# Moving the overflow block of a mixture of experts from the end of the expert loop to its middle

## The chip, the cores and the metric

The kernel runs on one core of a Trainium2 chip. The metric is the device time of one execution in microseconds; of several runs the median is taken. A second number is the span of the one execution that was profiled, from its first to its last recorded instruction.

## What is computed

The reference is one encoder block over 1024 tokens of width 1024: two attention branches, a gated merge, a layer norm, and then a mixture of 16 experts with a second layer norm. The change touches only the mixture. Each token picks one group of four experts and two experts in it, so there are 2048 token-expert pairs, and the outputs are added with the token's weights:

```python
y = jnp.zeros_like(u)
for e in range(N_EXPERTS):
    h = jax.nn.silu(u @ w_gate[e]) * (u @ w_up[e])
    y = y + comb[..., e:e + 1] * (h @ w_down[e])
```

The kernel computes only the pairs that were chosen. With these inputs the reference's own routing gives the experts 0 to 15 these numbers of tokens: 38, 69, 18, 17, 46, 151, 122, 119, 188, 61, 143, 180, 218, 177, 195, 306.

## The kernel before, in words

Tokens of one expert are gathered in blocks of 128 rows. Every expert has a first block; a second one is computed only if it has more than 128 tokens (here experts 5, 8 and 10 to 15; expert 15 needs a third). Blocks past an expert's second go on a list that is worked out on the chip (`overflow_list`, L1500). The first entry of that list gets a step of its own after the sixteen experts, with a weight load whose expert number is read from a register (`w_dyn`, L1627); further entries would be handled by a loop after it (L1738), which here has no pass.

All matrix products are made in three passes: each operand is split into a rounded high part and the remainder (`halves`, L200; the split of a 128x1024 weight piece is a copy on ScalarE, `ewh`, and a subtraction on VectorE, `ewl`), and `mm3` (L141) multiplies low by high, high by low and high by high.

For a block the work is: gather the tokens' rows from memory (`gather`, L1538, an indirect DMA of GpSimd into `xg`); transpose them on TensorE and split them (`transpose_x`, L1544, tiles `pxt`, `xh`, `xl`); gate and up (`gate_up`, L1565: 24 matmuls into `pgu`, then silu on ScalarE and a product on VectorE into `sg`); transpose the hidden activations (`hidden`, L1582, tiles `pht`, `hh`, `hl`); down (`down`, L1591: 12 matmuls into two banks `pdn`); scale (two VectorE operations into `ot`, L1614); and add the rows to the sums in memory (L1615, an indirect DMA of GpSimd into `acc_d`). Where a block is left out, one or two stand-in matmuls (L1576, L1606) fill its banks.

Each scatter adds to the same tensor `acc_d`, so each waits until the one before it has landed. There are two `ot` tiles, so an `ot` is written only once the scatter before last has landed.

An expert's weights are 3 MB in six pieces of 512 KB (`load_expert`, L1409): pieces 0 to 3 for gate and up, 4 and 5 for down. SyncE's queue issues them in order. Two pools hold the raw pieces and their splits, 16 slots (`L`) and 14 (`X`); successive steps use them by turns, so even steps use `X` and odd ones `L`.

The order of the work inside the loop is written out by hand, and the scheduler keeps it on all engines (`manual_schedule`, L1685). The loop runs over steps, and in each over the letters of one string (L37):

```python
ORDER = 'A4B0bC1cDEPe2FG35g'
```

In step e: `A` transposes the hidden activations of e-1; `B` and `C` are gate and up of e's two blocks, `b` and `c` their silu and product; `D` and `F` transpose the two blocks of e+1; `E` and `G` are the downs of e-1's two blocks, `e` and `g` their scaling and scatter; `P` issues the gathers of e+3; the digits 0 to 3 split pieces of e+1's weights, 4 and 5 the last two pieces of e's. Before the change step 16 is the overflow block, and pass 17 only finishes it. After the loop the sums are read back (L1758), normalised and written out.

Of the kernel before, what the change touches and what calls it, by code (L numbers as in the profile page):

```python
# [25 lines left out]
T = 1024  # L26
# [4 lines left out]
NE = 16  # L31
# [55 lines left out]
def block_kernel(ctx: ExitStack, tc, a, out):  # L87
    nc = tc.nc
    V, S, G, PE = nc.vector, nc.scalar, nc.gpsimd, nc.tensor
    dma = nc.sync.dma_start  # L90
    ET = mybir.EngineType
# [9 lines left out]
    def s2(name, tag, shape=(128, 512), dt=FT):  # L101
        return sb.tile(list(shape), dt, name=name, tag=tag, bufs=HALVES[tag])
# [727 lines left out]
    A = {}  # L830
# [574 lines left out]
    ew, first_gather = {}, []  # L1405
# [71 lines left out]
    idxg = cp.tile([128, 129], U32, name="idxg")  # L1477
    idxs = cp.tile([128, 129], U32, name="idxs")
# [7 lines left out]
    wtab = cp.tile([128, 129], FT, name="wtab")  # L1486
# [10 lines left out]
    lsti = cp.tile([128, 40], I32, name="lsti")  # L1497
    cnti = cp.tile([128, 16], I32, name="cnti")
# [44 lines left out]

    def transpose_x(xg, xh=None, xl=None):  # L1544
        if xh is None:
            xh, xl = s4("xh", "wh", dt=FR), s4("xl", "wl", dt=FR)
        for hf in range(2):
            p = bank("pxt", "tp")
            for k in range(4):
                PE.transpose(p[:, k * 128:k * 128 + 128], xg[:, (hf * 4 + k) * 128:(hf * 4 + k) * 128 + 128], ident)  # L1550
            t = slice(hf * 512, hf * 512 + 512)
            copy(xh[:, t], p)
            sub(xl[:, t], p, xh[:, t])
        return xh, xl
# [10 lines left out]
    def gate_up(w, x, sg, cond_=None):  # L1565

        xh, xl = x
        p = bank("pgu", "lg")

        def some():  # L1570
            for k in range(KC):
                ws = slice((k % 2) * 512, (k % 2) * 512 + 512)
                wh, wl = w[k // 2]
                mm3(p, xh[:, k * 128:k * 128 + 128], xl[:, k * 128:k * 128 + 128], wh[:, ws], wl[:, ws], k == 0, k == KC - 1)

        only(cond_, some, lambda: PE.matmul(p, w[0][0][:, 512:640], w[0][0][:, 0:512], start=True, stop=True))  # L1576
        yield
        S.activation(sg, p[:, 0:256], AF.Silu)
        V.tensor_tensor(sg, sg, p[:, 256:512], op=OP.mult)
        yield  # L1580

    def hidden(sg, n):  # L1582
        p = bank("pht", "av", (128, 256 * n))
        for k in range(2 * n):
            PE.transpose(p[:, k * 128:k * 128 + 128], sg[:, k * 128:k * 128 + 128], ident)
        hh, hl_ = s2("hh", "pt", (128, 256 * n), FR), s2("hl", "pt", (128, 256 * n), FR)
        copy(hh, p)
        sub(hl_, p, hh)
        return [(hh[:, 256 * b:256 * b + 256], hl_[:, 256 * b:256 * b + 256]) for b in range(n)]

    def down(w, h, wcol, isc, cond_=None, cond_p=None):  # L1591
        hh, hl_ = h
        ot = s4("ot", "b")
        p = [bank("pdn", "mm") for _ in range(2)]

        def some():
            for f in range(2):
                fs = slice(f * 512, f * 512 + 512)
                for k in range(2):
                    hs = slice(k * 128, k * 128 + 128)  # L1600
                    wh, wl = w[4 + k]
                    mm3(p[f], hh[:, hs], hl_[:, hs], wh[:, fs], wl[:, fs], k == 0, k == 1)

        def none():
            for f in range(2):
                PE.matmul(p[f], hh[:, 0:128], w[4][0][:, 0:512], start=True, stop=True)  # L1606

        only(cond_, some, none)
        yield

        def finish():
            for f in range(2):
                fs = slice(f * 512, f * 512 + 512)
                V.scalar_tensor_tensor(ot[:, fs], p[f], wcol, g2r[f], op0=OP.mult, op1=OP.mult)  # L1614
            G.indirect_dma_start(out=acc_d, out_offset=bass.IndirectOffsetOnAxis(ap=isc, axis=0), in_=ot, in_offset=None,  # L1615
                                 compute_op=OP.add)

        where(cond_p and cond_p(), finish)
        yield
# [14 lines left out]
    def prefetch(e):  # L1634
        for b in range(2 if e < NE else 0):
            xg[e, b] = gather(idxg[:, e * 8 + b:e * 8 + b + 1], second(e) if b else None)
        if e == NE:
            xg[e, 0] = gather(ic0[:, 0:1])

    def transposed(e, b):  # L1640
        if (e, b) in xg:
            x = xg.pop((e, b))
            h, l = s4("xh", "wh", dt=FR), s4("xl", "wl", dt=FR)
            where(several(e) if b else None, lambda: transpose_x(x, h, l))
            xt[e, b] = h, l

    def several(e, engines=(ET.PE, ET.Activation, ET.DVE)):

        return nc.values_load(cnti[0:1, e:e + 1], engines=list(engines), min_val=0, max_val=T) > 128

    def load(e, q):
        if e <= NE:
            if q == 0:
                if e == NE:
                    e_r = nc.values_load(lsti[0:1, 16:17], engines=[ET.SP], min_val=0, max_val=NE - 1)
                gens[e] = load_expert((lambda q: a["w_exp"][e, :, q * 1024:q * 1024 + 1024]) if e < NE else lambda q: w_dyn(e_r, q),
                                      "LX"[(e + 1) % 2])
            ew[e] = next(gens[e])

    gens = {}  # L1660
    copy(cnti, cnt16, V)
# [23 lines left out]
    man = tc.manual_schedule(engines={ET.PE, ET.DVE, ET.Activation, ET.Pool, ET.SP})  # L1685
    man.__enter__()


    def gu(e, b):
        if e > NE or (e == NE and b):  # L1690
            return iter(())
        if b == 0:
            sgs[e] = s2("sg", "sg")
        if b or e == NE:
            counts[e] = nc.values_load(cnti[0:1, e:e + 1] if e < NE else lsti[0:1, 32:33], engines=[ET.PE], min_val=0, max_val=T)
        return gate_up(ew[e], xt.pop((e, b)), sgs[e][:, b * 256:b * 256 + 256],
                       counts[e] > 128 * b if b or e == NE else None)

    def dn(e, b):
        if e < 0 or (e == NE and b):  # L1700
            return iter(())
        if e == NE:
            return down(ew[e], hs_[e][b], wo0, ic0[:, 1:2], counts[e] > 0,
                        lambda: nc.values_load(lsti[0:1, 32:33], engines=[ET.DVE, ET.Pool], min_val=0, max_val=T) > 0)
        col = e * 8 + b
        return down(ew[e], hs_[e][b], wtab[:, col:col + 1], idxs[:, col:col + 1], counts[e] > 128 if b else None,
                    (lambda: several(e, (ET.DVE, ET.Pool))) if b else None)

    for e in range(NE + 2):
        for n, c in enumerate(ORDER):  # L1710
            if c == "P":
                prefetch(e + 3)
            if c == "A" and 0 < e:
                hs_[e - 1] = hidden(sgs.pop(e - 1), 2 if e <= NE else 1)
            if c in "BC":
                g = gu(e, "BC".index(c))
                next(g, None)
            if c in "bc":
                next(g, None)
            if c in "DF":  # L1720
                transposed(e + 1, "DF".index(c))
            if c in "EG":
                d = dn(e - 1, "EG".index(c))
                next(d, None)
            if c in "eg":
                next(d, None)
            if c in "012345":
                q = int(c)
                ee = e if q >= 4 else e + 1
                if ee > 1:  # L1730
                    load(ee, q)

    held[0] = None
    man.__exit__(None, None, None)
# [108 lines left out]
```

## Time and profile before

| quantity | value |
|---|---|
| runs of the kernel before | 1376.50, 1386.26, 1388.22 us, median 1386.26 us |
| the profiled execution | 1377.23 us, its span 1375.4 us |
| mean granted TensorE clock in it | 0.957 |
| gate and up of step 0 begin | 1048.4 us into the span |
| the last scatter lands | 1342.9 us |
| scatters | 24 of experts' blocks, 1 of the overflow block |

The profile has, beside a page for the whole execution, views that can be cut to a stretch of time: the busy time of each engine in a list of windows; the instructions of one engine in order of time, with the idle time ahead of an instruction and what ended it in brackets; and the chain of work that ended last, followed back from the last instruction. In a row of the timeline the first number is the start in microseconds from the beginning of the span, the second the duration. A matmul's duration overlaps with the next one's, so costs on TensorE are taken from start to start.

### The profile page before, as it was taken

The numbers are of one execution on the slowest core, as the hardware profiler recorded it, in microseconds if no ns is written. First come the engines' busy times: TensorE is split into PE (matmuls) and PEld (weight loads), VectorE is DVE, ScalarE is ACT, GpSimd is POOL, SyncE is SP. The second block draws the span as 40 slices with busy tenths as digits, with TensorE's granted clock in tenths as the row PEclk, the third lists the DMA queues.
The fourth block names the chain that finished last, engine by engine and source line by source line (L and its number), as shares of the span: only waits on it lengthen the run. The fifth ranks groups of instructions, "written<-read, shape, count | busy, mean of one in ns | idle before, by whom it ended". The sixth has DMA issues, their size and how long they took to land. (4 is left out here: it accounts for less than half of the span.)

```text
span 1375.4 us, 18536 instructions
## 1 busy us (share of the span) xinstructions
PE 1246.5 (91%) x6216; PEld 978.6 (71%) x6231; DVE 960.0 (70%) x2096; ACT 673.9 (49%) x1198; POOL 124.3 (9%) x154
## 2 busy tenths in 40 slices
PE   7999999999999999998889898999986888999950
PEld 6876678877777777667667777787874766788840
DVE  6537699783447668655676768887798677877736
ACT  4536662224785545445746556434224455654415
POOL 1000000000000001001001100000002222333120
PEclk9999999999999999999989998999997999999985
DMA  9212452123124317564445522674436788989856
GB/s 368 91 32 70 149 183 75 47 72 117 61 74 145 131 55 242 188 184 127 147 136 153 163 69 67 231 240 158 178 107 230 249 288 244 320 289 311 245 86 251
DMA packets 108487, 225.92 MB, mean 164 GB/s; under 512 B 33104, under 2 KB 39648, under 8 KB 108384
## 3 DMA queue, kind: packets, MB, share of 16 engines
q1 hardware_dynamic: 67952, 164.22, 33.9%
q0 software_dynamic: 35824, 52.03, 14.0%
q10 hardware_dynamic: 4608, 8.39, 1.9%
q8 instruction: 53, 0.87, 0.2%
q14 instruction: 50, 0.41, 0.1%
HBM read 169.94 MB, written 54.58 MB: 163 GB/s over the span
## 5 line engine op out<-in xcount | busy, mean ns | idle before, releaser
L142 PE MATMUL pj<-uh,wl 128*128 128x512 f32 x544 | 220.7, 406 | 1.8 <-ACT bkr L132 0.8
L145 PE MATMUL pj<-ul,wh 128*128 128x512 f32 x544 | 216.2, 398 | 0.0
L146 PE MATMUL pj<-uh,wh 128*128 128x512 f32 x544 | 215.8, 397 | 0.0
L128 DVE TENSOR_TENSOR ewl<-raw,ewh 128x1024 fp32r<-128x1024 f32 x102 | 122.7, 1219 | 35.8 <-ACT ewh L132 30.2
L132 ACT ACTIVATE ewh<-raw 128x1024 fp32r<-128x1024 f32 x102 | 105.5, 1056 | 60.8 <-DMA raw<-w_exp 60.4
L142 PEld LDWEIGHTS pj<-uh,wl 128*128 128x128 f32 x544 | 102.6, 189 | 35.1 <-issue 10.2
L146 PEld LDWEIGHTS pj<-uh,wh 128*128 128x128 f32 x544 | 102.4, 188 | 26.1 <-issue 5.6
L145 PEld LDWEIGHTS pj<-ul,wh 128*128 128x128 f32 x544 | 102.7, 189 | 23.6 <-issue 5.1
L132 ACT ACTIVATE pth<-ptr 128x512 fp32r<-128x512 f32 (+1 forms) x120 | 65.7, 551 | 71.2 <-PE ptr L793 40.0
L128 DVE TENSOR_TENSOR ptl<-ptr,pth 128x512 fp32r<-128x512 f32 (+1 forms) x120 | 75.4, 634 | 23.6 <-ACT pth L132 22.9
L142 PE MATMUL pgu<-ewh,xl 128*128 128x512 f32 x200 | 81.4, 407 | 1.0 <-DVE xl L128 0.8
L793 PE MATMUL ptr<-ident,P 128*128 128x128 f32 x432 | 73.0, 286 | 8.4 <-DVE ptl L128 7.1
L146 PE MATMUL pgu<-ewh,xh 128*128 128x512 f32 x200 | 79.4, 397 | 0.0
L145 PE MATMUL pgu<-ewl,xh 128*128 128x512 f32 x200 | 79.4, 397 | 0.0
L765 ACT ACTIVATE P<-P,mx 128x128 f32<-128x128 f32 (+7 forms) x64 | 49.4, 772 | 39.9 <-DVE mx L762 36.7
L1615 POOL DMA_INDIRECT acc_d<-ot,idxs x24 | 47.5, 1980 | 198.4 <-DVE ot L1614 135.8
L793 PEld LDWEIGHTS ptr<-ident,P 128*128 128x128 f32 x432 | 52.3, 146 | 16.6 <-DVE ptl L128 8.0
L128 DVE TENSOR_TENSOR wl<-raw,wh 128x512 fp32r<-128x512 f32 x68 | 44.9, 686 | 22.8 <-ACT wh L132 22.6
L780 ACT ACTIVATE P<-P,mx 128x128 f32<-128x128 f32 (+3 forms) x64 | 49.4, 772 | 21.8 <-DVE mx L778 20.7
L758 PE MATMUL plg<-ak,aq 64*128 64x512 f32 (+4 forms) x288 | 58.2, 375 | 1.3 <-DVE mx L762 1.3
L444 DVE SCALAR_TENSOR_TENSOR sc<-relu,iw,sc 128x512 f32<-128x512 f32 (+3 forms) x70 | 45.4, 654 | 18.0 <-ACT relu L439 16.1
L142 PE MATMUL po<-woh,mxl 128*128 128x512 f32 x128 | 52.8, 412 | 3.0 <-DVE r L1210 3.0
(443 smaller groups left out, 2910.2 us busy)
## 6 DMA issues: line engine op xcount, KB each, us to landing
raw<-w_exp SPq DMA_DIRECT2D x102, 512.0 KB
raw<-w_main SPq DMA_DIRECT2D x68, 256.0 KB
adaw<-ada_b SPq DMA_DIRECT2D x32, 512.0 KB
adaw<-ada_a SPq DMA_DIRECT2D x16, 512.0 KB
gates_d<-gt SPq DMA_DIRECT2D x32, 256.0 KB
gate<-gates_d SPq DMA_DIRECT2D x32, 256.0 KB
xt<-xT SPq DMA_DIRECT2D x8, 512.0 KB
bv_d<-bvs SPq DMA_DIRECT2D x16, 256.0 KB
```

The lines of the kernel that those rows point to most:

```text
L128: e.tensor_tensor(o, i0, i1, op=OP.subtract)
L132: return S.activation(o, i, AF.Copy)
L142: i = PE.matmul(o, wl, xh, start=first, stop=False)
L145: PE.matmul(o, wh, xl, start=False, stop=False)
L146: e = PE.matmul(o, wh, xh, start=False, stop=last)
L444: V.scalar_tensor_tensor(acc, r[:, :n], w, acc, op0=OP.mult, op1=OP.add)
L758: i = PE.matmul(p[:, :n], q[a_][r, qs], k[b_][r, c0:c0 + n], start=m == 0, stop=m == 2)
L765: S.activation(P[:, :L], P[:, :L], AF.Exp, bias=mx_[:, 0:1], scale=-1.0, accum_out=mx_[:, 1:2])
L780: S.activation(P[:, :L], P[:, :L], AF.Exp, bias=mx[:, 0:1], scale=-1.0, accum_out=mx[:, 1:2])
L793: leads(PE.transpose(p[:, c:c + 128], Ps[s][:, kb * 128:kb * 128 + 128], ident))
L1615: G.indirect_dma_start(out=acc_d, out_offset=bass.IndirectOffsetOnAxis(ap=isc, axis=0), in_=ot, in_offset=None, compute_op=OP.add)
```

## The change

The steps get a sequence: positions 0 to 7 are experts 0 to 7, position 8 is the overflow block, positions 9 to 16 are experts 8 to 15. The functions that took an expert's number now take a position and look the expert up. The string of letters, the pools and what each step does are the same; by the position, not by the expert, a step uses `X` or `L`, so experts 8 to 15 swap pools.

```diff
+    SEQ = [*range(8), NE, *range(8, NE)]
+
+    def prefetch(i):
+        if i > NE:
+            return
+        e = SEQ[i]
         if e == NE:
-            xg[e, 0] = gather(ic0[:, 0:1])
...
+            xg[i, 0] = gather(ic0[:, 0:1])
+            return
+        for b in range(2):
+            xg[i, b] = gather(idxg[:, e * 8 + b:e * 8 + b + 1], second(e) if b else None)
...
-    def load(e, q):
-        if e <= NE:
+    def load(i, q):
+        if i <= NE:
+            e = SEQ[i]
             if q == 0:
                 if e == NE:
                     e_r = nc.values_load(lsti[0:1, 16:17], engines=[ET.SP], min_val=0, max_val=NE - 1)
-                gens[e] = load_expert((lambda q: a["w_exp"][e, :, q * 1024:q * 1024 + 1024]) if e < NE else lambda q: w_dyn(e_r, q),
-                                      "LX"[(e + 1) % 2])
-            ew[e] = next(gens[e])
+                gens[i] = load_expert((lambda q: a["w_exp"][e, :, q * 1024:q * 1024 + 1024]) if e < NE else lambda q: w_dyn(e_r, q),
+                                      "LX"[(i + 1) % 2])
+            ew[i] = next(gens[i])
...
-    for e in range(NE + 2):
+    for i in range(NE + 2):
         for n, c in enumerate(ORDER):
             if c == "P":
-                prefetch(e + 3)
-            if c == "A" and 0 < e:
-                hs_[e - 1] = hidden(sgs.pop(e - 1), 2 if e <= NE else 1)
+                prefetch(i + 3)
+            if c == "A" and 0 < i:
+                hs_[i - 1] = hidden(sgs.pop(i - 1), 1 if SEQ[i - 1] == NE else 2)
```

On GpSimd's queue at the end of the loop stood, before, the scatter of expert 15's first block, its second (behind a branch on `cnti`, the experts' token counts), and then the overflow's (its rows' numbers are in `ic_10498`, its branch reads `lsti`):

```order
L1615 DMA acc_d<-ot,idxs 1152x1024
L1649 TENSOR_LOAD cnti
L1535 COMPARE_AND_BRANCH
L1615 DMA acc_d<-ot,idxs 1152x1024
L1535 UNCONDITIONAL_BRANCH
L1535 ISA
L1535 UNCONDITIONAL_BRANCH
L1560 UNCONDITIONAL_BRANCH
L1704 TENSOR_LOAD lsti
L1535 COMPARE_AND_BRANCH
L1615 DMA acc_d<-ot,ic_10498 1152x1024
```

In the changed kernel the same place holds expert 15's two scatters and nothing more; the next row reads the number of passes of the loop after it:

```order
L1615 DMA acc_d<-ot,idxs 1152x1024
L1656 TENSOR_LOAD cnti
L1535 COMPARE_AND_BRANCH
L1615 DMA acc_d<-ot,idxs 1152x1024
L1535 UNCONDITIONAL_BRANCH
L1535 ISA
L1535 UNCONDITIONAL_BRANCH
L1746 TENSOR_LOAD lsti
```

The overflow's scatter has moved to GpSimd's queue between the gathers (`xg`) for position 12 and those for position 13:

```order
L1540 DMA xg<-u_d,idxg 128x1024
L1535 UNCONDITIONAL_BRANCH
L1535 ISA
L1535 UNCONDITIONAL_BRANCH
L1560 UNCONDITIONAL_BRANCH
L1713 TENSOR_LOAD lsti
L1535 COMPARE_AND_BRANCH
L1615 DMA acc_d<-ot,ic_10498 1152x1024
L1535 UNCONDITIONAL_BRANCH
L1535 ISA
L1535 UNCONDITIONAL_BRANCH
L1540 DMA xg<-u_d,idxg 128x1024
```

So a scatter of one block stands where expert 8's used to, and every later scatter comes one place later in the chain.

On SyncE's queue the register load of the overflow's expert number (from `lsti`) now stands ahead of position 8's first weight piece:

```order
L217 DMA raw<-w_exp 128x1024
L1663 TENSOR_LOAD lsti
L1663 ISA x2
L217 ISA
L217 DMA raw<-w_exp 128x1024
L217 ISA
L217 DMA raw<-w_exp 128x1024
```

Before, the same rows stood ahead of the loads of step 16, the last of the loop.

More of the change, by code (lines that the diff above doesn't have):

```diff
@@ L1632, in second, with transposed @@
         return nc.values_load(cnti[0:1, e:e + 1], engines=[ET.Pool], min_val=0, max_val=T) > 128
-    def prefetch(e):
-        for b in range(2 if e < NE else 0):
-            xg[e, b] = gather(idxg[:, e * 8 + b:e * 8 + b + 1], second(e) if b else None)
-        if e == NE:
-            xg[e, 0] = gather(ic0[:, 0:1])
-    def transposed(e, b):
-        if (e, b) in xg:
-            x = xg.pop((e, b))
+    SEQ = [*range(8), NE, *range(8, NE)]
[3 more added lines that the diff above has]
+        e = SEQ[i]
+        if e == NE:
+            xg[i, 0] = gather(ic0[:, 0:1])
+            return
+        for b in range(2):
+            xg[i, b] = gather(idxg[:, e * 8 + b:e * 8 + b + 1], second(e) if b else None)
+    def transposed(i, b):
+        if (i, b) in xg:
+            x = xg.pop((i, b))
             h, l = s4("xh", "wh", dt=FR), s4("xl", "wl", dt=FR)
-            where(several(e) if b else None, lambda: transpose_x(x, h, l))
-            xt[e, b] = h, l
+            where(several(SEQ[i]) if b else None, lambda: transpose_x(x, h, l))
+            xt[i, b] = h, l
     def several(e, engines=(ET.PE, ET.Activation, ET.DVE)):
         return nc.values_load(cnti[0:1, e:e + 1], engines=list(engines), min_val=0, max_val=T) > 128
-    def load(e, q):
-        if e <= NE:
+    def load(i, q):
+        if i <= NE:
+            e = SEQ[i]
             if q == 0:
@@ L1686, in block_kernel, with gu, dn @@
     man.__enter__()
-    def gu(e, b):
-        if e > NE or (e == NE and b):
+    def gu(i, b):
+        if i > NE or (SEQ[i] == NE and b):
             return iter(())
+        e = SEQ[i]
         if b == 0:
-            sgs[e] = s2("sg", "sg")
+            sgs[i] = s2("sg", "sg")
         if b or e == NE:
[L1695 to L1700, printed above, removed]
+            counts[i] = nc.values_load(cnti[0:1, e:e + 1] if e < NE else lsti[0:1, 32:33], engines=[ET.PE], min_val=0, max_val=T)
+        return gate_up(ew[i], xt.pop((i, b)), sgs[i][:, b * 256:b * 256 + 256],
+                       counts[i] > 128 * b if b or e == NE else None)
+    def dn(i, b):
+        if i < 0 or (SEQ[i] == NE and b):
             return iter(())
+        e = SEQ[i]
         if e == NE:
-            return down(ew[e], hs_[e][b], wo0, ic0[:, 1:2], counts[e] > 0,
+            return down(ew[i], hs_[i][b], wo0, ic0[:, 1:2], counts[i] > 0,
                         lambda: nc.values_load(lsti[0:1, 32:33], engines=[ET.DVE, ET.Pool], min_val=0, max_val=T) > 0)
         col = e * 8 + b
-        return down(ew[e], hs_[e][b], wtab[:, col:col + 1], idxs[:, col:col + 1], counts[e] > 128 if b else None,
+        return down(ew[i], hs_[i][b], wtab[:, col:col + 1], idxs[:, col:col + 1], counts[i] > 128 if b else None,
                     (lambda: several(e, (ET.DVE, ET.Pool))) if b else None)
-    for e in range(NE + 2):
+    for i in range(NE + 2):
         for n, c in enumerate(ORDER):
             if c == "P":
-                prefetch(e + 3)
-            if c == "A" and 0 < e:
-                hs_[e - 1] = hidden(sgs.pop(e - 1), 2 if e <= NE else 1)
+                prefetch(i + 3)
+            if c == "A" and 0 < i:
+                hs_[i - 1] = hidden(sgs.pop(i - 1), 1 if SEQ[i - 1] == NE else 2)
             if c in "BC":
-                g = gu(e, "BC".index(c))
+                g = gu(i, "BC".index(c))
                 next(g, None)
@@ L1720, in block_kernel @@
             if c in "DF":
-                transposed(e + 1, "DF".index(c))
+                transposed(i + 1, "DF".index(c))
             if c in "EG":
-                d = dn(e - 1, "EG".index(c))
+                d = dn(i - 1, "EG".index(c))
                 next(d, None)
@@ L1728, in block_kernel @@
                 q = int(c)
-                ee = e if q >= 4 else e + 1
-                if ee > 1:
-                    load(ee, q)
+                ii = i if q >= 4 else i + 1
+                if ii > 1:
+                    load(ii, q)
     held[0] = None
```

## Prediction

> **What bounds the kernel now.** I read the page first, to find the stage that the change touches; then the busy times cut at the starts of the expert steps; then the rows of TensorE, ScalarE and VectorE inside two of these steps; last the chain of work that ended last, for the end of the stage.
>
> ```profile
> span 1375.4 us, 18536 instructions
> ...
> PE 1246.5 (91%) x6216; PEld 978.6 (71%) x6231; DVE 960.0 (70%) x2096; ACT 673.9 (49%) x1198; POOL 124.3 (9%) x154
> ...
> DMA  9212452123124317564445522674436788989856
> ...
> raw<-w_exp SPq DMA_DIRECT2D x102, 512.0 KB
> ```
>
> The expert stage is the last fifth of the span. TensorE is busy 91% over the whole kernel, but the DMA digits climb to 8 and 9 in just this stage, where 102 pieces of 512 KB (six for each of 17 steps) come in beside the gathers and the scatters. So two things may limit a step, and they have to be told apart step by step. I cut the stage where each step's first transposes (pht) start on TensorE; the columns are the stretch, busy time and count of each engine, granted clock, DMA share, GB/s. The rows are steps 5, 6, 8, 9, 10, 11, 15, 16 and what follows up to the landing of the last scatter.
>
> ```profile
> core 0: us, PE busy (x) PEld busy (x) DVE busy (x) ACT busy (x) POOL busy (x), PEclk, DMA share, GB/s
> 1121.01:1138.20 17.19, 16.63 (x75) 13.58 (x74) 12.06 (x16) 9.69 (x13) 4.42 (x4) 0.95 0.72 233
> 1138.20:1157.52 19.32, 14.81 (x62) 11.82 (x61) 14.08 (x17) 8.24 (x11) 6.21 (x3) 0.82 0.97 318
> 1169.45:1185.90 16.45, 15.77 (x76) 12.81 (x75) 12.06 (x16) 8.18 (x12) 4.82 (x4) 1.00 1.02 355
> 1185.90:1200.18 14.28, 13.91 (x71) 11.18 (x69) 12.93 (x17) 10.67 (x15) 7.54 (x4) 1.00 0.90 327
> 1200.18:1216.52 16.34, 16.34 (x84) 13.71 (x83) 11.47 (x16) 6.96 (x11) 4.32 (x4) 1.00 0.96 295
> 1216.52:1235.12 18.60, 18.60 (x94) 15.56 (x92) 14.41 (x19) 11.51 (x16) 6.78 (x4) 1.00 0.76 278
> 1290.90:1308.65 17.75, 17.75 (x85) 14.74 (x84) 12.70 (x16) 8.19 (x12) 3.05 (x2) 1.00 0.56 137
> 1308.65:1320.03 11.38, 11.38 (x54) 9.40 (x53) 7.82 (x10) 2.88 (x4) 2.35 (x2) 1.00 0.61 115
> 1320.03:1342.91 22.88, 4.90 (x15) 3.47 (x13) 3.15 (x5) 0.38 (x1) 4.66 (x3) 0.67 0.51 81
> ```
>
> From step 10 on TensorE is busy without a gap, so TensorE is the bound there; in step 6 it idles 4.5 us with the DMA at 0.97. The last 22.88 us belong to neither: TensorE works 4.90 us of them and the DMA stands at 0.51. The chain that ended last names their owner:
>
> ```profile
> 1307.15 8.22 DMA acc_d<-ot,idxs
> 1316.12 6.06 DMA acc_d<-ot,idxs
> 1322.95 6.12 DMA acc_d<-ot,idxs
> 1329.79 6.23 DMA acc_d<-ot,idxs
> 1336.79 6.12 DMA acc_d<-ot,ic
> 1343.78 3.33 DMA r<-acc_d
> ```
>
> These are the scatters of expert 14's two blocks, expert 15's two, and the overflow block (ic). Each starts about 0.7 us after the one before has landed, and the read of the sums follows the last. So the end of the stage is five scatters in a row, and the overflow's is the last link.
>
> **The change, part by part.** I write 8' to 17' for the steps of the changed kernel: 8' is the overflow, 9' is expert 8, 17' the closing pass. Steps 0 to 7 keep their work, except that the gather fetched ahead for position 8 is one instead of two. The amounts of matmuls, splits, loads and scatters are the same in sum. So the price is how long the inserted step keeps expert 11 back, less what the end gets shorter. First the pieces of a TensorE step, from step 10 (48 matmuls of gate and up, transposes of 8 tiles, 12 matmuls of down, transposes, 2 stand-in matmuls, next step):
>
> ```profile
> 1200.18 0.60 PE L1585 MATMUL pht<-ident,sg 128*128 128x128 f32 x4
> 1200.53 0.48 PE L142 MATMUL pgu<-ewh,xl 128*128 128x512 f32 x1
> 1211.55 1.04 PE L1550 MATMUL pxt<-ident,xg 128*128 128x128 f32 x8
> 1212.35 0.48 PE L142 MATMUL pdn<-ewh,hl 128*128 128x512 f32 x1
> 1215.17 1.03 PE L1550 MATMUL pxt<-ident,xg 128*128 128x128 f32 x8
> 1215.96 0.71 PE L1606 MATMUL pdn<-ewh,hh 128*128 128x512 f32 x2
> 1216.52 0.60 PE L1585 MATMUL pht<-ident,sg 128*128 128x128 f32 x4
> ```
>
> From start to start: pht 0.35, one block's gate and up 11.02 / 2 = 5.51, a transposed block 0.80, a down 2.82, two stand-ins 0.56. The other limit is seen in steps 6 and 8, on ScalarE (the splits of the next expert's pieces 0 and 1, with the wait for their landing), VectorE (the scaling of the first block's result) and TensorE:
>
> ```profile
> 1143.46 1.06 ACT L132 ACTIVATE ewh<-raw 128x1024 fp32r<-128x1024 f32 x1 [3.08 <-DMA raw<-w_exp]
> 1148.10 1.06 ACT L132 ACTIVATE ewh<-raw 128x1024 fp32r<-128x1024 f32 x1 [3.30 <-DMA raw<-w_exp]
> 1176.52 1.06 ACT L132 ACTIVATE ewh<-raw 128x1024 fp32r<-128x1024 f32 x1 [4.04 <-DMA raw<-w_exp]
> 1180.34 1.06 ACT L132 ACTIVATE ewh<-raw 128x1024 fp32r<-128x1024 f32 x1 [2.48 <-DMA raw<-w_exp]
> ```
>
> ```profile
> 1151.86 1.40 DVE L1614 SCALAR_TENSOR_TENSOR ot<-pdn,wtab,g 128x512 f32<-128x512 f32 x2
> 1184.10 1.40 DVE L1614 SCALAR_TENSOR_TENSOR ot<-pdn,wtab,g 128x512 f32<-128x512 f32 x2
> ```
>
> ```profile
> 1152.65 0.79 PE L142 MATMUL pdn<-ewh,hl 128*128 128x512 f32 x1 [4.51 <-DVE ot L1614]
> 1185.29 0.77 PE L1606 MATMUL pdn<-ewh,hh 128*128 128x512 f32 x2 [0.68 <-DVE ot L1614]
> ```
>
> Piece 1 of the next expert lands 9.9 us after the start of step 6 and 10.9 after that of step 8. Both engines work in order, so the result ot, written two to four microseconds after that split, is late too, and TensorE cannot start the second down before its banks are read. With two blocks (step 8) TensorE has gate-and-up work meanwhile and loses 0.68 us. With one block (step 6) it loses 4.51 us. The overflow has one block: the inserted step lacks the cover, and it moves the one-block expert 9 to an even position, like step 6.
>
> *Step 8'.* TensorE alone: 0.35 + 5.51 + 0.80 + 2.82 + 0.80 + 0.56 = 10.8 us. The landing path of step 8 (the same pieces, the same down of expert 7) gives 16.45. I take 15.0: that path, less the 0.4 us of one sg multiply that VectorE no longer has ahead of ot and about 1 us for the spared gather. *Step 9'* (expert 8, two blocks; down of the overflow, one): TensorE alone 0.35 + 11.02 + 0.80 + 2.82 = 15.0; the nearest measured, step 5, has 17.19; I take 15.3, as the long gate-and-up covers the landings. *Step 10'* (expert 9, down of expert 8): the same work as step 9; TensorE alone 0.35 + 5.51 + 0.24 + 0.80 + 2.82 + 0.80 + 2.82 = 13.3 (0.24 for one stand-in), step 9 itself 14.28, but step 6, with the same blocks at an even position, 19.32. I take 15.5, near step 9, whose work it is, with a quarter of the way to step 6. *Step 11'* is step 10, 16.34; step 5's 17.19 is its upper bound.
>
> Sum: 15.0 + 15.3 + 15.5 + 16.3 = 62.1 us from 1169.45, where before expert 11 began 47.07 us after it (1216.52). Expert 11 is **15.0 us late**; low 10.8 + 15.0 + 13.3 + 16.3 = 55.4, so 8.3; high 16.45 + 17.19 + 19.32 + 17.19 = 70.2, so 23.1. From there TensorE is the bound as before (18.60 a step) and keeps the delay.
>
> *The end.* Behind expert 15's second scatter nothing is left: 1336.79 - 1329.79 = 7.0 us saved. Step 16' has no further block to transpose: 0.8. Expert 14's first scatter took 8.22 us beside the last weight piece against 6.06 to 6.23 of the later ones; that piece lands earlier now: 0 to 2.1, I take 1.0. In all **8.8 us saved** (7.0 to 9.9). What hides expert 15's last downs is the chain: two downs and their scaling are 2 x 2.82 + 2 x 1.40 = 8.4 us, and TensorE idled 18 of the last 22.88. Without this cover up to 8.4 us would be due again.
>
> The register load of the expert's number moves on SyncE's queue from ahead of the last weights to ahead of position 8's; weights of positions 7 and 8 queue behind it. Nothing here prices it alone; zero to one raw's issue time is within the bounds above. On GpSimd's queue the overflow's gather and scatter take the place of expert 8's, and expert 8's come one step later.
>
> The net is 15.0 - 8.8 = **+6.2 us**, from 8.3 - 9.9 = -1.6 to 23.1 - 7.0 = +16.1. The profiled execution took 1377.2 us (span 1375.4 and 1.8 around it), so its like would be 1383.4; the median of the runs shown is 1386.3, 9 us above it, and so I forecast **1392.5 us**.
>
> On the clock, step 6's row has a granted 0.82 after its wait of 4.51 us, and step 8's 1.00 after 0.68. The Trainium skill ("TensorE: Matmul & The Clock Gate", "What's actually happening") says that an idle window of about 3.4 us halves the clock until a busy window has passed. The trace agrees in direction, and by that rule a wait over 3.4 us in step 10' costs some 1.7 us more (an estimate from that page), a wait of 2 us nothing; the sum by it would stay at +6.2, and rival one would come as a jump.
>
> **The rivals.** *One, slower:* step 10' turns into step 6. The place is the second down of expert 8, behind the scaling of its first block, behind piece 1 of expert 10. TensorE gets there 10.5 us into the step (0.35 + 5.51 + 0.24 + 0.80 + 2.82 + 0.80), and from the split to the free bank takes 1152.65 - 1148.10 = 4.55 us: it begins once the piece lands later than 6 us into the step, and each microsecond more costs one (my 15.5 has it land at 8, step 6 had 9.9). With all high bounds this is +16 us, 1402. For it: step 6 has just these blocks, and the DMA stood at 1.02 and 0.90 in steps 8 and 9, so there is little room for one more expert's 3 MB. Against it: step 6 followed a step at 0.72 with an empty stretch before its burst, and step 9 ran the same work in 14.28. *Two, it evens out:* the weights are far enough ahead for 8' and 10' to run at TensorE's pace: -1.6 us, 1385. For it: DMA shares of 0.76 and 0.56 in steps 11 and 15. Against: pieces 0 and 1 came 4.04 and 2.48 us late just where the step is put in. *Three, the change doesn't do what it says at the end:* another transfer, say expert 15's last weights, ends last and only the 0.8 us are saved: 15.0 - 0.8 = +14.2, 1400. Against: the last weights are due a step and a half before the end, and step 15 shows 0.56 of DMA.
>
> **How the numbers follow.** Forecast 0.58, rival one 0.18, two 0.18, three 0.06. About 1% (14 us) is what a measurement of this kernel can tell from no change. Over 1% slower is above 1400.1: two thirds of rival one, half of three and a thin edge of the forecast, 0.17. Over 1% faster lies 12 us below the low bound; 0.03 is left for what I have not seen. Within 1%: 0.80. The low and high of the sum are 1385 and 1402; the runs shown reach from 1376.5 to 1388.2, so the range is pulled down to 1380 and ends at 1402.
>
> **What would show it.** Right: the last four scatters lie end to end, the last one carries idxs and the read of the sums follows it; expert 11's first transposes lie about 62 us behind those of step 8'; TensorE waits for ot in 8' and 10'. Wrong: step 8' at 11 us or under; step 10' at 19; a gap between the last scatters of more than 0.7 us; a step after 12' longer than 18.6.

## The result, and the profile after

| | median us | runs | kernel before, same chip | ratio, 95% interval |
|---|---|---|---|---|
| changed kernel | 1398.80 | 6 | 1380.49 | 1.0115 [1.0081, 1.0149] |
| the same, a second time (last experiment) | 1395.28 | 12 | 1386.48 | 1.0060 [1.0029, 1.0091] |

The change makes the kernel slower, by 16 us in the first measurement and 8 us in the second; a ratio weighs all runs and is not the quotient of the two medians. The intervals overlap between 1.0081 and 1.0091. The forecast was +6.2 us, and "within 1%" was given 0.80. The first measurement lies beyond 1%, the second within. Both medians are inside the range. The profiled execution of experiment 2 was one of that program's slow ones, so only its ratio is used, and not the step of 25.9 us that the expectation of experiment 6 names.

The page of the changed kernel, profiled at 1397.35 us:

```profile
span 1395.5 us, 18542 instructions
...
PE 1259.0 (90%) x6216; PEld 988.2 (71%) x6231; DVE 960.3 (69%) x2096; ACT 674.9 (48%) x1198; POOL 124.3 (9%) x154
```

The amounts of work are the same. But one trap lies in comparing the two spans: 20.1 us of difference are not 20.1 us of the change. The expert stage's first gate and up begins at 1048.42 before and at 1057.28 here, 8.9 us later, in code that the change doesn't touch; over all the profiled executions below it begins between 1046.5 and 1063.9. Steps 0 to 7, whose code is the same too, took 121.0 us before and 118.0 here, and 116.7 to 124.6 in the other executions. So I compare from the start of position 8 to the start of the read of the sums: 1169.45 to 1343.78 before, **174.3 us**; 1175.26 to 1363.80 after, **188.5 us**: +14.2.

The busy times of the changed kernel, cut at each step's first transposes (columns as in the prediction): 8', 9', 10', 11', 14', 16', and the closing pass up to the landing of the last scatter.

```profile
core 0: us, PE busy (x) PEld busy (x) DVE busy (x) ACT busy (x) POOL busy (x), PEclk, DMA share, GB/s
...
1175.26:1192.24 16.98, 12.36 (x59) 9.41 (x58) 10.77 (x13) 8.93 (x13) 3.92 (x4) 0.92 1.02 333
1192.24:1209.15 16.91, 16.76 (x72) 13.56 (x70) 10.34 (x14) 6.83 (x11) 4.31 (x3) 0.88 0.70 250
1209.15:1227.88 18.73, 15.57 (x70) 12.36 (x71) 15.69 (x20) 10.79 (x15) 7.72 (x4) 0.91 0.98 336
1227.88:1244.21 16.33, 16.33 (x83) 13.70 (x82) 10.09 (x14) 6.96 (x11) 3.66 (x4) 1.00 0.88 258
...
1281.42:1301.25 19.83, 19.08 (x93) 15.51 (x92) 13.31 (x18) 11.01 (x15) 2.07 (x2) 1.00 1.02 321
1319.86:1336.67 16.81, 16.81 (x77) 13.90 (x76) 8.49 (x12) 3.27 (x6) 3.05 (x2) 1.00 0.48 95
1336.67:1362.92 26.25, 6.65 (x29) 4.71 (x27) 4.79 (x7) 0.60 (x1) 5.46 (x4) 0.75 0.53 80
```

Expert 11 begins 16.98 + 16.91 + 18.73 + 16.33 = 68.95 us after position 8, where it began 47.07 us after it before: **21.9 us late** (forecast 15.0). Step 14' adds 1.2 (19.83 for 18.6). The end, from the start of 16' to the read, is 1363.80 - 1319.86 = 43.94 us, where it was 1343.78 - 1290.90 = 52.88 (from step 15): **8.9 us saved** (forecast 8.8). 21.9 + 1.2 - 8.9 = +14.2.

TensorE's waits in 8' and 10' and two matmuls at the start of 9', early and a few microseconds on:

```profile
1187.55 1.27 PE L1550 MATMUL pxt<-ident,xg 128*128 128x128 f32 x8 [1.52 <-issue]
1191.08 1.36 PE L1606 MATMUL pdn<-ewh,hh 128*128 128x512 f32 x2 [2.26 <-DVE ot L1614]
...
1193.10 0.63 PE L145 MATMUL pgu<-ewl,xh 128*128 128x512 f32 x1
...
1196.61 0.39 PE L145 MATMUL pgu<-ewl,xh 128*128 128x512 f32 x1
...
1222.21 1.27 PE L1550 MATMUL pxt<-ident,xg 128*128 128x128 f32 x8 [3.14 <-issue]
```

In 10' TensorE does not wait where step 6 did, ahead of the second down, but one piece earlier, ahead of the second block's transposes (pxt). "issue" names no releaser; the other engines' rows show one. ScalarE in 10', the splits of expert 10's pieces 0 and 1, the copy of the first transposed block, the split of piece 2:

```profile
1217.39 1.06 ACT L132 ACTIVATE ewh<-raw 128x1024 fp32r<-128x1024 f32 x1 [4.56 <-DMA raw<-w_exp]
...
1218.63 1.06 ACT L132 ACTIVATE ewh<-raw 128x1024 fp32r<-128x1024 f32 x1
...
1219.85 1.08 ACT L132 ACTIVATE xh<-pxt 128x512 fp32r<-128x512 f32 x2
1222.12 1.06 ACT L132 ACTIVATE ewh<-raw 128x1024 fp32r<-128x1024 f32 x1 [1.19 <-DMA raw<-w_exp]
```

VectorE: the scaling of 8', and in 10' the second halves of the splits of pieces 0 and 1 and of the first transposed block:

```profile
1190.19 1.41 DVE L1614 SCALAR_TENSOR_TENSOR ot<-pdn,wtab,g 128x512 f32<-128x512 f32 x2 [2.13 <-DMA acc_d<-ot,idxs]
...
1218.49 1.23 DVE L128 TENSOR_TENSOR ewl<-raw,ewh 128x1024 fp32r<-128x1024 f32 x1 [2.80 <-ACT ewh L132]
...
1219.96 1.22 DVE L128 TENSOR_TENSOR ewl<-raw,ewh 128x1024 fp32r<-128x1024 f32 x1
...
1221.43 1.28 DVE L128 TENSOR_TENSOR xl<-pxt,xh 128x512 fp32r<-128x512 f32 x2
```

The transposes start at 1222.21, in the middle of the two xl (1221.43 to 1222.71): their bank pair is read last by xl. The chain is landing of piece 0 (1217.39, 8.2 us into the step), piece 1 right behind it (split at 1218.63, 9.5 us in), their subtractions on VectorE (ewl), xl behind these, banks free, transposes. The kernel before has this wait too, in step 4, where a one-block expert is also followed by one with two blocks:

```profile
1118.55 1.48 PE L1550 MATMUL pxt<-ident,xg 128*128 128x128 f32 x8 [2.00 <-issue]
```

VectorE's first row above shows another wait in 8': it had its operands, but the tile ot was still being read by an earlier scatter, 2.13 us.

SyncE's queue of weight pieces around 9' and 10' (start, time from the first to the end of the last, count):

```profile
1169.56 19.70 SPq L217 DMA_DIRECT2D raw<-w_exp  x12
...
1208.12 15.31 SPq L217 DMA_DIRECT2D raw<-w_exp  x12
```

From 1189.26 to 1208.12 SyncE issues no piece. The first one at 1208.12 is piece 4 of expert 9 (position 10), 15.9 us into 9'; in the kernel before, the piece 4 for position 10 goes out 6.5 us into step 9 (at 1192.37). Its slot was free then by a split of the same expert's piece 0. In the changed kernel it is given a slot that holds the overflow's down weights, and these are read until the end of 9'. So expert 9's last two pieces go out together with expert 10's.

Last, the chain at the end (start, us, what):

```profile
1325.00 6.09 DMA acc_d<-ot,idxs
...
1335.17 6.97 DMA acc_d<-ot,idxs
...
1342.87 6.17 DMA acc_d<-ot,idxs
...
1349.81 6.23 DMA acc_d<-ot,idxs
...
1356.78 6.14 DMA acc_d<-ot,idxs
...
1363.80 3.37 DMA r<-acc_d
```

The scatter with ic is gone from the end; the last four are expert 14's two (from 1335.17) and expert 15's two, with some 0.7 us between them, and the read follows.

### The profile page after: what moved, and what is told of

It is laid out like the page before. It is cut to its first block, busy times and chain, and to the rows that moved or that the text cites. A ratio compares the mean times of both kernels' runs of the same rounds, so it can differ in the third digit from the quotient of the medians.

```text
span 1395.5 us, 18542 instructions
## 1 busy us (share of the span) xinstructions
PE 1259.0 (90%) x6216; PEld 988.2 (71%) x6231; DVE 960.3 (69%) x2096; ACT 674.9 (48%) x1198; POOL 124.3 (9%) x154
## 5 line engine op out<-in xcount | busy, mean ns | idle before, releaser
L145 PEld LDWEIGHTS pj<-ul,wh 128*128 128x128 f32 x544 | 103.5, 190 | 23.9 <-issue 5.2
L444 DVE SCALAR_TENSOR_TENSOR sc<-relu,iw,sc 128x512 f32<-128x512 f32 (+3 forms) x70 | 45.4, 654 | 17.9 <-ACT relu L439 15.9
```

The lines of the kernel that those rows point to most:

```text
L145: PE.matmul(o, wh, xl, start=False, stop=False)
L444: V.scalar_tensor_tensor(acc, r[:, :n], w, acc, op0=OP.mult, op1=OP.add)
```

## The experiments

Each ratio is against the kernel before on the same chip. In the first four expectations the letters stand for readings of the price: A takes it to come from late weight pieces where a step has too little TensorE work to cover them, B from the inserted expert's traffic wherever it stands; C is a third reading, with its number where it is named.

**1. The overflow before expert 15** (in the changed kernel):

```
-    SEQ = [*range(8), NE, *range(8, NE)]
+    SEQ = [*range(15), NE, 15]
```

> The overflow stands between experts 14 and 15 instead of between 7 and 8; nothing else differs. Theory A (the price of the inserted step is set by the cover at its place: where the weights run behind, a one-block step costs what their landing takes, among two-block steps it costs TensorE's own work, 10 to 11 us, and the end saves 8 to 9 us or more): the closing pass begins 9.6 us later than before, only three scatters are left in the last chain, so the end comes 21 us after it instead of 34; net -3.6 us, ratio 0.997. Theory B (one more expert's traffic costs the same 22 us wherever it is put): +13 us, ratio 1.009 or more. Theory C (experts behind the inserted step pay for swapping pools): only expert 15 swaps, so as A.

Measured: 0.9999 [0.9966, 1.0032]. From position 8 to the read 173.2 us, 174.3 before. B's 1.009 is out; A's 0.997 lies at the edge. The place matters: moved past one expert the overflow costs nothing, moved past eight it costs 8 to 16 us.

**2. The overflow between experts 11 and 12**, both with two blocks:

```
-    SEQ = [*range(8), NE, *range(8, NE)]
+    SEQ = [*range(12), NE, *range(12, NE)]
```

> The overflow stands between experts 11 and 12, among two-block experts; nothing else differs. Theory A (cover): the two steps that replace one take 13.1 + 15.8 us where 18.6 stood, so +10.3, and the end saves 8.9: net +1.4 us, ratio 1.001, and TensorE shows no wait over 1 us in the inserted step. Theory B (traffic, the place does not matter): +13 us, ratio 1.009 or more. Theory C (swapped pools): experts 12 to 15 swap, half of the eight, so about half of the change's price, +8 us, 1.006.

Measured: 1.0089 [1.0051, 1.0127]. A falls in the form that it had: two-block neighbours do not make the insertion free.

**3. Experts 9 and 10 swapped**, so that step 10' has two blocks:

```
-    SEQ = [*range(8), NE, *range(8, NE)]
+    SEQ = [*range(8), NE, 8, 10, 9, *range(11, NE)]
```

> The changed kernel with experts 9 and 10 exchanged, so that the one-block expert 9 stands at an odd position and the two-block expert 10 at the even one. Theory A (cover, with the burst of weights at the start of even steps): the wait ahead of expert 8's second down goes away; the steps of 9, 10 and 11 take 49 us instead of 53.7: 4.5 us less than the changed kernel, ratio to the kernel before 1.008 instead of 1.0115. Theory B (traffic alone): no difference from the changed kernel, 1.0115. Theory C (pools): no difference either.

Measured: 1.0074 [1.0040, 1.0107]; steps 15.9, 17.0, 18.3, 13.8. The number is A's against the first measurement of the change, but it is no gain against the second (1.0060). Nor do the rows decide: experts 9 to 11 took 50.6 us together, and in the two profiles of the changed kernel 53.7 and 50.6. Undecided.

**4. No weights for the overflow.** It multiplies with the weights of the expert before it, so that none of its six pieces is loaded or split; what it adds to the sums then comes from expert 7's weights. Experts 8 to 15 keep the pools of the kernel before.

```
+            if e == NE:
+                ew[i] = ew[i - 1]
+                return
...
-                                      "LX"[(i + 1) % 2])
+                                      "LX"[(e + 1) % 2])
```

> The changed kernel, but the overflow step at position 8 loads no weights of its own: it reads those of the step ahead, so the overflow block's contribution is computed with expert 7's weights; its 3 MB of loads and six pairs of splits are left out, and experts 8 to 15 keep the pools that they had before the change. Theory A (the landing of the weights prices the step): step 8' takes TensorE's 11 us, step 10' shows no wait over 1 us, expert 11 begins 10 to 11 us later than before instead of 22, net +2 us, ratio 1.001. A theory that the price is the step's own work on TensorE, ScalarE and VectorE or its scatter: step 8' stays at 15 us or more, net +12 us or more, 1.009.

Measured: 1.0063 [1.0035, 1.0090]; steps 14.3, 16.1, 14.5, 16.3, together 61.2 us, so expert 11 is still 14.1 us late. Neither number came; the interval lies between them and just touches 1.009. Most of the delay needs no weights of the overflow. By the prediction's pieces TensorE's work alone takes 55.4 us for these four steps, 8.3 us more than before; at the end that work lay under the scatters. The other 5.8 us are waits and a lower clock (0.95 and 0.94 in 8' and 9') that stay without the weights. The longest is again for ot, in 8':

```profile
1192.70 1.36 PE L1606 MATMUL pdn<-ewh,hh 128*128 128x512 f32 x2 [2.31 <-DVE ot L1614]
```

**5. The slot given back.** Four stand-in matmuls read the overflow's down weights where a second block's down would read them. They take a bank of their own and some 0.5 us of TensorE, and the slot of piece 4 two positions on is then the one that its own piece 0 frees, as in the kernel before.

```
+        if e == NE and b:
+            p = bank("pdn", "mm")
+            for w in ew[i][4] + ew[i][5]:
+                PE.matmul(p[:, 0:256], w[:, 0:128], hs_[i][0][0], start=True, stop=True)
+            return iter(())
```

> The changed kernel with four stand-in matmuls (under 1 us of TensorE) after the overflow's down, so that its down weights are read at the point of the step at which a second block would read them; piece 4 of the expert two positions behind the overflow then gets the slot that its own piece 0 frees, as in the kernel before, and not one that the overflow's down frees. Theory S (the slot): in the changed kernel that piece is issued 15.9 us into step 9' in place of about 6.5, and pieces 0 and 1 of expert 10 queue behind it; with the slot restored step 10' falls from 18.7 us to 15 to 16, and the ratio from 1.0115 to about 1.009. Theory B (traffic): the pieces of three megabytes more are too many for 10' wherever piece 4 stands; step 10' stays at 18 or above and the ratio at 1.0115 to 1.012.

Measured: 1.0061 [1.0038, 1.0085]. In its trace SyncE's queue, alone in the middle of 9' (which began at 1178.25), and ScalarE's splits of pieces 0 and 1 in 10' (from 1195.70):

```profile
1185.27 0.33 SPq L217 DMA_DIRECT2D raw<-w_exp  x1
```

```profile
1201.18 1.06 ACT L132 ACTIVATE ewh<-raw 128x1024 fp32r<-128x1024 f32 x1 [3.29 <-DMA raw<-w_exp]
...
1202.41 1.04 ACT L132 ACTIVATE ewh<-raw 128x1024 fp32r<-128x1024 f32 x1
```

```profile
1195.70:1210.10 14.40, 14.03 (x71) 11.18 (x70) 13.03 (x16) 8.02 (x12) 7.16 (x4) 1.00 0.94 311
```

Piece 4 goes out 7.0 us into 9', piece 0 lands 5.5 us into 10', and 10' takes 14.40 us, nearly TensorE's own time. So the slot does decide when piece 4 goes out. What it is worth is another matter (experiment 12); 9' takes 17.45 us here, 0.5 to 0.8 more than without the stand-ins.

**6. The same stand-ins with the overflow between experts 11 and 12.**

> The overflow between experts 11 and 12, with the same four stand-ins. Without them this place gave 1.0089 and a step 14 of 25.9 us, where piece 4 of the expert two positions behind the overflow also got the overflow's slot. Theory S: step 14 falls to about 18.6 us (TensorE's pace), and the ratio by 0.004 to 0.005, to about 1.004 or 1.005. Theory B: the ratio stays at 1.009 and step 14 well above 20 us.

Measured: 1.0101 [1.0061, 1.0141], against 1.0089 without them; step 14 took 21.6 us, well above 18.6. Theory S's numbers did not come, but the run does not test it. A load of the closing pass stands on SyncE's queue ahead of pieces 3 and 4 of position 14 and waits 14.0 us (the last column is the longest wait), so that these go out only 12.6 and 13.1 us into 13, though their slots are free by then:

```profile
SPq L138 <- PE pxt L1550: 14.0, 1, 14.0
```

**7. The kernel before without the overflow's scaling and scatter.**

```
-            return down(ew[e], hs_[e][b], wo0, ic0[:, 1:2], counts[e] > 0,
-                        lambda: nc.values_load(lsti[0:1, 32:33], engines=[ET.DVE, ET.Pool], min_val=0, max_val=T) > 0)
+            g = down(ew[e], hs_[e][b], wo0, ic0[:, 1:2], counts[e] > 0, None)
+            next(g)
+            return iter(())
```

> The kernel before, with the overflow's scaling and scatter left out (rows of the overflow block are not added to the sums). Theory A (the chain at the end, five scatters one behind another): 7.0 us less, ratio about 0.995. Rival: another transfer ends as late and the ratio stays at 0.999 to 1.001.

Measured: 0.9946 [0.9921, 0.9971], 7.5 us less. The chain of that run ends one link sooner:

```profile
1329.23 6.23 DMA acc_d<-ot,idxs
...
1336.18 6.25 DMA acc_d<-ot,idxs
...
1343.38 3.35 DMA r<-acc_d
```

The last link is worth its 7 us. From the start of step 10 to the read that run took 136.7 us, the kernel before 143.6.

**8. Two-block experts at the even positions, one-block at the odd.**

```
-    SEQ = [*range(8), NE, *range(8, NE)]
+    SEQ = [0, 1, 8, 2, 10, 3, 11, 4, 12, 6, 13, 7, 14, 9, 5, NE, 15]
```

> The same experts in another order: experts with two blocks at the even positions, those with one at the odd ones, and the overflow last but one. Theory P (parity): an even step issues about ten weight pieces and an odd one two, so a two-block step has to stand where the ten come in; TensorE idles 19.2 us in steps 0 to 11 of the kernel before, and most of this goes: 8 to 17 us less, ratio 0.988 to 0.994. Rival: the order doesn't matter, since the sum of the pieces is the same and the DMA is the bound of the first twelve steps: ratio 0.998 to 1.002.

Measured: 0.9886 [0.9838, 0.9933], 16 us faster than the kernel before. All waits of TensorE from the start of step 2 into step 15 (engine, line, waited for: us in all, times, longest):

```profile
PE pdn L1606 <- PEq L1535: 3.6, 6, 0.7
PE pdn L142 <- DVE ot L1614: 2.0, 3, 1.1
PE pdn L1606 <- DVE ot L1614: 1.0, 2, 0.6
```

**9. The same with the overflow in the middle**, at the odd position 9:

```
-    SEQ = [*range(8), NE, *range(8, NE)]
+    SEQ = [0, 1, 8, 2, 10, 3, 11, 4, 12, NE, 13, 6, 14, 7, 5, 9, 15]
```

> Two-block experts at the even positions and one-block ones at the odd ones, as in the run that alternated them, but with the overflow in the middle, at the odd position 9, in place of position 15. Theory P (parity): what the move costs is decided by the step that the overflow pushes the one-block experts into; at an odd step between two-block ones it costs nothing beside TensorE's time for it, which is there at any place: ratio 0.985 to 0.992, as with the overflow last but one (0.9886). Theory B (traffic of an inserted expert costs wherever it stands): 0.004 to 0.009 above that, 0.993 to 0.998.

Measured: 0.9874 [0.9840, 0.9908]. The overflow in the middle costs nothing here beside its place last but one (0.9886).

**10. The other parity**: two-block experts at the odd positions.

```
-    SEQ = [*range(8), NE, *range(8, NE)]
+    SEQ = [0, 8, 1, 10, 2, 11, 3, 12, 4, 13, 6, 14, 7, 5, 9, 15, NE]
```

> The contrast: two-block experts at the odd positions and one-block ones at the even ones, overflow last. Theory P: each even step from 2 on has ten or eleven weight pieces to bring in beside one block's work and takes 16 to 19 us in place of about 14, so 15 to 25 us more than the order with the other parity: ratio 1.000 to 1.007. Rival (any alternation evens the load out): 0.986 to 0.992, as there.

Measured: 1.0005 [0.9976, 1.0035], 16 us slower than the order of 8. Its two worst even steps (4 and 10), an odd one (11), and the longest wait of TensorE between the starts of steps 2 and 15:

```profile
1119.60:1140.90 21.30, 16.39 (x70) 13.42 (x69) 15.15 (x19) 9.32 (x13) 7.86 (x4) 0.84 0.97 324
...
1222.20:1241.20 19.00, 15.16 (x70) 12.54 (x69) 13.95 (x18) 9.41 (x13) 7.85 (x4) 0.91 0.97 331
1241.20:1257.50 16.30, 15.68 (x75) 12.80 (x74) 10.47 (x15) 8.25 (x11) 2.66 (x3) 1.00 0.74 196
```

```profile
PE pxt L1550 <- issue: 10.2, 3, 4.9
```

The wait is the one of step 10' (pxt behind xl behind the first pieces), in even steps with one block. Theory P holds for the whole: by the starts on SyncE's queue an even step of the orders of 8 and of this one issues ten pieces and an odd one two, and in these two orders only the two-block steps cover the ten throughout. It does not hold for each step: the even ones from 2 on took 14.5 to 21.3 us, and three of the seven waited so.

**11. A one-block expert last:**

```
-    SEQ = [*range(8), NE, *range(8, NE)]
+    SEQ = [0, 1, 8, 2, 10, 3, 11, 4, 12, 6, 13, 7, 14, NE, 5, 15, 9]
```

> Two-block experts at the even positions up to 14, the overflow at 13, then the two-block expert 15 at position 15 and the one-block expert 9 last. Theory A (the end is a chain of scatters of some 7 us each, behind the last down): with one block last, TensorE's closing pass has one down in place of two, and one scatter less hangs behind the last down: 3 to 7 us less than with a two-block expert last: ratio 0.983 to 0.987. Rival: the chain is as long, since the scatters of expert 15 queue there as well: 0.988 to 0.990.

Measured: 0.9887 [0.9851, 0.9922]. The ratio is the rival's, though its interval reaches into A's range. The rows are the rival's as well: from the start of the closing pass to the read 24.9 us, in the order of 8 23.9. The scatters queue whoever comes last.

**12. The changed kernel again:**

> The changed kernel once more, to set the four stand-ins (1.0061) against it on more runs. Theory S (the slot of piece 4): 1.010 to 1.013, so that the stand-ins gained 5 us. Rival: the changed kernel lies at 1.006 to 1.008 as well and the stand-ins gained nothing that can be measured.

Measured: 1.0060 [1.0029, 1.0091]. The rival's number, so the stand-ins' gain cannot be measured in the whole time. From position 8 to the read the run with them took 183.0 us, this one 183.9. The same three steps 8' to 10' of this execution, TensorE's wait in 10', and the split of piece 0:

```profile
1175.98:1191.50 15.52, 11.92 (x59) 9.17 (x58) 10.53 (x13) 7.99 (x12) 4.61 (x4) 1.00 1.01 333
1191.50:1208.20 16.70, 16.55 (x72) 13.38 (x70) 10.61 (x14) 7.41 (x11) 4.56 (x3) 0.90 0.75 265
1208.20:1223.80 15.60, 13.95 (x69) 11.19 (x70) 14.04 (x18) 10.49 (x15) 7.22 (x4) 1.00 0.98 326
```

```profile
1219.76 1.27 PE L1550 MATMUL pxt<-ident,xg 128*128 128x128 f32 x8 [1.64 <-issue]
```

```profile
1214.94 1.06 ACT L132 ACTIVATE ewh<-raw 128x1024 fp32r<-128x1024 f32 x1 [2.91 <-DMA raw<-w_exp]
```

Piece 4 of expert 9 is as late as in the first profile (15.7 us into 9'), but the burst behind it came in faster: piece 0 landed 6.7 us into 10' and not 8.2. The wait halved, the granted clock stayed at 1.00, and 10' took 15.60 us in place of 18.73. Expert 11 was 17.1 us late; 17.1 + 0.7 (14') - 8.4 (the end) = +9.4, and 183.9 us are +9.5.

## Why the prediction was right or wrong, point by point

| step, us | forecast | first profile | second | slot given back | no weights |
|---|---|---|---|---|---|
| 8' | 15.0 | 16.98 | 15.52 | 15.05 | 14.3 |
| 9' | 15.3 | 16.91 | 16.70 | 17.45 | 16.1 |
| 10' | 15.5 | 18.73 | 15.60 | 14.40 | 14.5 |
| 11' | 16.3 | 16.33 | 16.30 | 16.30 | 16.3 |
| sum | 62.1 | 68.95 | 64.1 | 63.2 | 61.2 |

- **The frame held.** A step more on TensorE's path, a shorter end, and nothing else of size: +14.2 and +9.5 us are made up by these terms, in both profiles. That both medians lie in the range is in part luck. The forecast stood on three runs with a median of 1386.3; with three more the kernel before lies at 1380.49, and the same sum on that would have ended at 1396.6, below the first median of 1398.80.
- **The end: right.** 8.8 forecast, 8.9 and 8.4 measured in the two profiles. Its lesser terms came too: 0.9 for 0.8 in 16' (16.81 against 17.75), and expert 14's first scatter took 6.97 us in place of 8.22, 1.25 for 1.0. (Its lower bound of 7.0 leaves out the 0.8; by its own terms it is 7.8.) Taking the last link alone away gave 7.5 (experiment 7; forecast 7.0). The four last scatters end to end, idxs last, as said. Rival three is out.
- **8': near in the second profile, 2 us too low in the first, and one of the two waits missed.** 15.0 stood against 15.52 and 16.98, the latter above its upper bound of 16.45; no run prices the "about 1 us for the spared gather" in it. The forecast had the whole wait come from the landing of piece 1. The first, 1.52 us (1.24 in the second profile), is of that kind, ahead of the transposes. The second, 2.26 (2.25), is the tile ot, held by an earlier scatter: VectorE's row names it. The prediction had looked at what VectorE is queued behind, not at whether its output tile was free. Nor is it the scatter before last that holds the tile, as said above the prediction: that one had landed at 1178.04. It is the last one, expert 6's, which began at 1178.83 and landed 11.2 us later. The code takes an ot tile for a second block that is left out as well, so behind a one-block expert the next scaling needs the tile of the scatter just ahead.
- **9': mis-sized, 15.3 against 16.9 and 16.7.** TensorE does not wait there (busy 16.76 of 16.91). Its granted clock is 0.88 and 0.90: the matmuls run at 0.63 us until about 1196, then at 0.39. This is a price of 8' that is paid in 9', 1.5 to 1.8 us (16.55 and 16.76 against the 15.0 of the pieces). The prediction let the clock into 10' alone, and only for one wait over 3.4 us. The Trainium skill ("TensorE: Matmul & The Clock Gate", "What's actually happening") speaks of an idle window of about 3.4 us; here no single wait was that long, and 1.52 and 2.26 us with 1.3 us of transposes between were enough in 8', 3.14 us in 10', while 1.64 us in the second profile was not. The measurement decides. But it is not the length of a wait either: in the first profile one of 2.74 us in step 6 left the clock at 1.00. What fits is how much TensorE worked in one stretch of a fixed grid: the clock's changes in this profile (at 1127.94, 1131.35, 1189.38, 1196.20 and 1223.51 among others) all lie whole multiples of 3.41 us apart. In the stretch that ends in the waits of 8' it was busy 1.32 us, and the next two ran at half the clock; the wait of step 6 lies across two stretches, with 2.13 and 1.95 us busy:

```profile
1160.12 0.50 PE L142 MATMUL pdn<-ewh,hl 128*128 128x512 f32 x1 [2.74 <-DVE ot L1614]
```

```profile
1155.25:1158.66 3.41, 2.13 (x10) 1.43 (x8) 2.26 (x4) 2.31 (x4) 0.00 (x0) 1.00 1.03 311
1158.66:1162.07 3.41, 1.95 (x8) 1.61 (x9) 3.20 (x5) 1.23 (x2) 1.07 (x1) 1.00 1.03 420
...
1185.97:1189.38 3.41, 1.32 (x9) 0.84 (x8) 2.08 (x3) 1.88 (x4) 0.00 (x0) 1.00 1.02 321
1189.38:1192.79 3.41, 1.71 (x5) 1.25 (x6) 2.60 (x4) 2.57 (x4) 0.92 (x1) 0.50 1.02 417
```

  The stretch ahead of the lowered clock in 10' (1220.10 to 1223.51) has 1.28 us busy. The 1.64 us of the second profile lie across two stretches as well, with 2.69 and 2.49 us busy.
- **10': the mechanism right but for its last link, the number in the second profile right (15.60 for 15.5).** The forecast had late pieces hold up VectorE's queue, and TensorE wait for the scaling (ot) ahead of the second down. The pieces and the queue were as said. But where the next expert has a second block, its transposes stand ahead of that down, and their banks are freed by xl, which stands ahead of ot on VectorE. In step 6, the pattern of the forecast, the next expert has one block; step 4 was the nearer pattern. So TensorE did not wait for ot in 10'. The size is hardly touched: from the split of piece 1 to these transposes took 3.58, 3.59 and 3.58 us (first profile, second, slot given back), and by the pieces TensorE gets there 9.7 us into the step, so the wait begins once piece 1 comes later than 6.1 us into it; the forecast had 6. It came at 6.7, 8.0 and 9.5 us (slot given back, second, first), where the forecast took 8, and the steps took 14.40, 15.60 and 18.73 us. That one execution met the 8 is luck: the forecast had put it a quarter of the way from step 9 to step 6, and knew nothing of the slot. The first two are a microsecond for a microsecond; between the last two the lower clock (0.91 for 1.00) adds the rest.
- **What was missed: the slot.** "The amounts are the same in sum" was true, but the loads are not at the same times: as the overflow has no second block, its down weights count as read earlier, the pool gives their slot to piece 4 of position 10, and that piece and the next go out half a step later, ahead of expert 10's. Shown in the traces (15.9 and 15.7 us into 9', 7.0 with the stand-ins). Against the run with the stand-ins 10' is 1.2 us longer in the second profile (15.60 against 14.40) and 4.3 in the first (18.73), each in one execution, so that the speed of the burst is in these differences too; in the whole time no difference could be measured (1.0060 and 1.0061).
- **14': missed.** "A step after 12' longer than 18.6" was to speak against the forecast, and came: 19.83 and 19.3. A load of the closing pass stands on SyncE's queue among the pieces for position 14, and waits for a slot that a transpose in 13' frees:

```profile
SPq L138 <- PE pxt L1550: 16.9, 2, 14.0
```

  These 14.0 us (the longest, third column) hold back pieces 3 and 4 of expert 13, issued 12.8 and 13.4 us into 13'; before, those of position 14 went out in 12 and 6.1 us into 13. That this costs the 0.7 to 1.2 us is argued and not shown: with experts 9 and 10 swapped (experiment 3) the two pieces go out just as late, 12.8 and 13.3 us into 13', and 14' takes 18.67 us. So the late issue alone does not make the step longer.
- **Rival one** gave +16, and the first profile comes near it: 10' at 18.73, by late pieces and VectorE's queue, though one link earlier than it said, and the four steps at 68.95 us of its 70.2. In the second profile it did not come. **Rival two** is out: 8' (10.8 by the pieces) took 14.3 to 17.0 us, and 10' (13.3) 14.4 to 18.7.
- **Open:** why the same kernel lay at 1.0115 and at 1.0060. 10' alone differs by 3.1 us and 8' by 1.5 between the two profiles, with the same order of loads, so the speed of the burst varies from execution to execution; what varies it was not found. Nor is the time of the place between experts 11 and 12 (1.0089 and 1.0101) settled, where the load of the closing pass holds the queue too (experiment 6).

The better version is neither kernel: alternating the experts by the number of their blocks gives 0.9886 with the overflow last but one and 0.9874 with it in the middle.

## What to carry to other kernels

Work that lies under a chain of transfers at the end is free there; moved to where the engine is the bound it costs its full time, and only what the chain loses comes back. In a loop over tile pools find out first in which steps the transfers really go out: here it was every second one, and matching the long steps to them was worth 16 us, as much as the worst place of the one step cost. Before calling a moved step "the same work", follow its tiles' slots, too: who gets them next, and when.

## What the runs showed of the hardware that was not expected

- The granted clock fell after two waits of 1.52 and 2.26 us with 1.27 us of transposes between (0.88 in the step that followed, matmuls of 0.63 us in place of 0.39), and stayed at 1.00 after a single one of 2.74 us. The busy time within one stretch of a fixed grid of 3.41 us tells these apart: 1.32 us against 2.13 and 1.95. Worked out from TensorE's rows of this stage in all fourteen profiles, a stretch at full clock with under 1.4 us busy was always followed by half the clock, one with over 2.0 never.
- A scatter beside a full burst of weights holds its tile long: the one that began at 1178.83 took 11.2 us, where those at the end take 6.1 to 6.3, and VectorE waited 2.13 us for ot in 8' at a DMA share of 1.02.
- Stretches of unchanged code moved by 8 us (steps 0 to 7: 116.7 to 124.6) and the start of the stage by 17 us (1046.5 to 1063.9) between executions, so two profiles were compared by stretch and not by span.
